# Gathered V rows and table blocks in separate pools, selection ended at slot 64, 58 table pairs beside the dots, high one-hots by one compare

## The chip, the cores and the metric

One Trainium2 chip (trn2), one of its NeuronCores. The metric is the device time of one execution in microseconds, lower is better. A NeuronCore has five engines that run their own instruction streams: TensorE (PE in the profile; PEld is its weight load), VectorE (DVE), ScalarE (ACT), GpSimd (POOL) and SyncE (SP), and 16 DMA engines that all of them share.

## The reference, cut to what matters

Two transformer-like blocks run over 256 tokens of 1024 numbers. The first (an mLSTM mixer, an MLP and a gated addition) and the first half of the second (forgetting attention, an RWKV-7 mixer, a layer norm) are not touched by the change. The last part is a product-key expert layer, `_peer`. Per block of 128 tokens:

```python
q = (xb @ w_q).reshape(t, PEER_HEADS, 2, PEER_HALF)
s = jnp.einsum('thpd,hpkd->thpk', q, sub_keys).astype(jnp.float32)
top_s, top_i = lax.top_k(s, K)                       # K = 16, 8 heads, 128 keys a half
cand_s = top_s[:, :, 0, :, None] + top_s[:, :, 1, None, :]
cand_i = top_i[:, :, 0, :, None] * PEER_N_KEYS + top_i[:, :, 1, None, :]
best_s, best_pos = lax.top_k(cand_s.reshape(t, PEER_HEADS, K * K), K)
idx = jnp.take_along_axis(cand_i.reshape(t, PEER_HEADS, K * K), best_pos, axis=-1)
gate = jax.nn.softmax(best_s, axis=-1).astype(xb.dtype)
h = jax.nn.gelu(jnp.einsum('thkd,td->thk', u_table[idx], xb), approximate=False)
return jnp.einsum('thk,thkd->td', gate * h, v_table[idx])
```

So each token picks 8 x 16 = 128 of 16384 experts; each pick is called a slot here. For every slot the dot of a row of U (1024 numbers, 4 KB) with the token gives a weight, and the output is the weighted sum of the same rows of V. A layer norm follows. All of it is float32.

## The kernel before, in words

The 256 tokens are two blocks, 0 and 1, of 128 tokens, one token per partition. The tail of the kernel has four stages; times are from the profile.

**Dots of block 0** (line 1507, to about 891 us) and **dots of block 1** (line 1590, 891 to 1147). A slot n gathers 128 rows of U, one per token, by an indirect DMA that GpSimd issues (`gather`, line 1376), and VectorE multiplies and sums them with the tokens in one instruction (`u_dot`, line 1404). For some slots of the early part TensorE does it instead (`u_mm`, line 1380, and `u_diag`). The row tiles come from `ub` (six tiles of 4 KB per partition) and, for block 1 and four slots of seven, from a tag `ust` of eight tiles in the pool `sec` (`u_tile`, line 1368). Beside the dots VectorE selects the experts of the heads to come (`select`, advanced in steps by `paced`). In block 1 the selection of the last six heads is spread to slot `SEL`. At that slot the pools `late` (the selection's) and `sec` are closed, and the one-hot tensor of block 1, `AT1`, is put in their place, 64 KB per partition. From then on rows have only the six tiles of `ub`.

**The dense product.** V isn't gathered for block 0, nor for the low half (columns 0 to 511) of block 1. There a weight matrix is built over all 16384 experts. An expert's index is 128 x high + low. For each token, the tensor `AT` holds at [low, token, high] the sum of weights; it is the product of a low one-hot and a weighted high one-hot over the token's 128 slots. ScalarE makes the low one-hots (`spread_low`, line 1425: four Squares and a Relu for a group of four tokens). `spread` (line 1432) does the rest for a group: VectorE compares the iota row with the high index and multiplies by the weight (line 1439, four instructions of 128x128, one per token), TensorE multiplies the two one-hots, ScalarE evicts. There are 32 groups per block. The matrix then multiplies blocks of the V table: a **pair** is 256 experts x 512 columns, 512 KB, and there are 64 pairs for each half of the columns. A float32 product of 128x128 by 128x512 is two passes on TensorE, so a pair is four passes for one token block.

- High half of V for block 0: `hload` (line 1556) loads a pair `wh`, `hdense` (line 1571) multiplies it and asks for the next. `H1` of the 64 pairs are asked for beside the dots of block 1, the others in the spreads of block 1 (line 1666). The tiles are from `wraw` (four tiles, through `h_tile`), two of a tag in `sec` for two of six pairs while it is open, and from `ub` after the dots (`late_h`).
- Low half of V for both blocks: the last stage, line 1721, 1216 to 1512 us: `vload` loads a pair `w`, `dense` multiplies it for block 0 and for block 1. The first six (`PRE`) come from `ub`; after them even pairs from `ub`, odd ones from `wraw`.
- High half of V for block 1: gathered. `v_load` (line 1452) gathers 128 half rows of 2 KB, two slots to one tile; `v_add` (line 1461) multiplies them by the weight and adds them on VectorE. Six are asked for ahead. 28 are added between the spreads of block 1 (from the fifth group on), 100 in the last stage. The tiles come from `wraw` up to the last stage, and from `ub` in it (`v_tile`, `paced_v`).

What sets the order: VectorE runs its instructions in the order written (`manual_schedule`, line 1237). For the other engines the tile framework works out an order when the kernel is built, in which an instruction or a load may stand ahead of ones that are written before it; it also hands out the tiles of a pool in that order, and sets the waits. On the chip each engine then runs its own list in order. So SyncE's list holds the loads of `wh` and `w`, GpSimd's the gathers, and a wait of one holds all behind it.

The end: after the adds, `low_half(0)` and `last_norm(0)` run beside the last six pairs of block 1, then `low_half(1)`, `last_norm(1)` and the output.

Of the kernel before, what the change touches and what calls it, by code (L numbers as in the profile page):

```python
# [18 lines left out]
S, D = 256, 1024  # L19
# [4 lines left out]
def block_kernel(ctx: ExitStack, tc: tile.TileContext, I, out):  # L24
# [7 lines left out]
    sm = ctx.enter_context(tc.tile_pool(name="sm", bufs=4, side="right"))  # L32
# [17 lines left out]
    def pb():  # L50
        return psB.tile([128, 512], F, tag="b", name="pb")
# [1380 lines left out]
    def spread(t, q, ns=128):  # L1432

        g = AT[t][:, q * 4:q * 4 + 4]
        ps = pb()
        for i in range(4):
            n = q * 4 + i
            e1 = gt_.tile([128, 128], F, tag="e1", name="e1")[:ns]
            V.tensor_scalar(e1, io[:ns], tr_all[t][:ns, 0, n:n + 1], tr_all[t][:ns, 2, n:n + 1],  # L1439
                            op0=OP.is_equal, op1=OP.mult)  # L1440
            T.matmul(ps[:, i * 128:(i + 1) * 128], lhsT=g[:ns, i], rhs=e1, start=True, stop=True)  # L1441
        A.activation(out=g, in_=ps.rearrange("p (t i) -> p t i", t=4), func=AF.Copy)


    vts, paced_v = {}, []

    def v_tile():
        if paced_v:
            return ub.tile([128, D], R, tag="u", name="v").bitcast(F)
        return h_tile("v")  # L1450

    def v_load(s):
        if not vts:
            w = v_tile()
            vts[1], v = w[:, 512:], w[:, :512]
        else:
            v = vts.pop(1)
        gather(v, vhalf, idx_v[1], s)
        return v
# [70 lines left out]
    gt_ = ctx.enter_context(tc.tile_pool(name="onehot", bufs=6, side="right"))  # L1530

    def h_tile(name):
        return wraw.tile([128, WF], F, tag="raw", name=name)[:, :D]
# [50 lines left out]
    SEL, LOW, HN = 83, 36, 38  # L1584

    H1 = 48
# [3 lines left out]
    for n in range(128):  # L1590
# [32 lines left out]
        if n > SEL:  # L1623
            for _ in range((n - SEL - 1) * 32 // (127 - SEL), (n - SEL) * 32 // (127 - SEL)):
                spread_next(spread_low, low1, 1)
# [5 lines left out]
    def vload(b):  # L1631
        if b >= PRE and b % 2:
            w = h_tile("w")
        else:
            w = ub.tile([128, D], R, tag="u", name="w").bitcast(F)
        wt[b] = w.rearrange("p (b c) -> p b c", b=2)
        nc.sync.dma_start(out=wt[b], in_=vtab[b * 256:(b + 1) * 256, 0:512].rearrange("(b p) c -> p b c", p=128))
# [40 lines left out]
    paced_v.append(1)  # L1678
# [93 lines left out]
```

## Time and profile before

| | |
|---|---|
| runs of the kernel before | median 1530.12 us of 3 (1524.57 to 1533.26) |
| the profiled execution | 1525.52 us device time, span 1523.7 us, mean granted clock 0.954 |
| busy, share of the span | PE 85%, DVE 65%, ACT 36%, POOL 29% |
| HBM read | 336.21 MB |
| chain, by engine | PE 52%, DMA 17%, DVE 13%, ACT 10%, issue 4%, POOL 2% |

The span runs from the first to the last instruction of one profiled execution; the device time has 1.8 us more. A row of a group view reads: line, engine, operation, tiles written and read, shape, count, then busy us and mean ns of one, then the engine's idle time just before these instructions and what ended it. "Granted clock" is TensorE's clock as granted, a share of 2.4 GHz. A tile's name is that in the code: `u` and `ust` are rows of U, `v` gathered half rows of V, `wh` and `w` pairs of the V table, `e` the high one-hot, `AT` the matrix, `jk` the dot.

### The profile page before, as it was taken

What the parts mean: (1) busy time and instruction counts of PE and PEld (TensorE: products, weight loads), DVE (VectorE), ACT (ScalarE), POOL (GpSimd) and SP (SyncE); (2) the same over time, 40 slices, a digit from 0 to 9 for tenths busy, and PEclk for the clock granted to TensorE, in tenths of its full rate; (3) what the DMA queues carried; (4) which work ended last, traced back from release to release, by engine and by line L of the source; (5) the groups of instructions that cost most, each with busy time, mean ns of one, the idle gap of its engine ahead of it and who ended that gap; (6) DMA issues with size and microseconds to landing.
All of it is one profiled execution on the core that took longest, in us unless ns stands there. A gap on an engine that the chain in (4) does not pass through costs nothing.

```text
span 1523.7 us, 20095 instructions
## 1 busy us (share of the span) xinstructions
PE 1297.5 (85%) x7068; PEld 1054.6 (69%) x7068; DVE 987.4 (65%) x2456; ACT 546.2 (36%) x1046; POOL 446.2 (29%) x420
## 2 busy tenths in 40 slices
PE   8999999999999999979987579955558988793955
PEld 7889899878987788869887568832226855462633
DVE  6778555576664766878999889998565943212123
ACT  6465544474556412312325964300097300000000
POOL 2000000000000000036787764565433564223231
PEclk9999999999999999989999789999999999896987
DMA  7435665655443300559999997799998776654732
GB/s 239 137 126 183 193 190 186 188 173 162 137 138 118 107 12 1 177 202 366 342 371 346 340 354 242 241 402 401 401 401 305 244 259 214 236 196 119 260 90 90
DMA packets 132820, 338.58 MB, mean 222 GB/s; under 512 B 11674, under 2 KB 15088, under 8 KB 132720
## 3 DMA queue, kind: packets, MB, share of 16 engines
q1 hardware_dynamic: 83680, 165.01, 33.0%
q0 software_dynamic: 48288, 170.98, 31.3%
q10 hardware_dynamic: 752, 1.31, 0.3%
q8 instruction: 56, 0.92, 0.3%
q14 instruction: 44, 0.36, 0.1%
HBM read 336.21 MB, written 1.05 MB: 221 GB/s over the span
## 4 chain that ended last, share of the span: by engine, by line
PE 52%; DMA 17%; DVE 13%; ACT 10%; issue 4%; POOL 2%; SPq 0%; DVEq 0%; ACTq 0%; POOLq 0%
DMA v<-in_peer_v_dram,idxv 9%; PE pa L217 7%; PE pa L219 7%; PE pa L218 7%; ACT AT L1429 5%; PE pa L1642 4%; DVE jk L1408 4%; PE pa L1396 3%; DMA u<-in_peer_u_dram,idxu 3%; PE pb L1441 2%; PE pb L217 2%; PE pb L219 2%; PE pb L218 2%; ACT AT L1430 2%; PE pa L1187 2%
## 5 line engine op out<-in xcount | busy, mean ns | idle before, releaser
L1642 PE MATMUL pa<-w,AT 128*128 128x512 f32 x512 | 235.4, 620 | 69.2 <-DMA w<-in_peer_v_dram 69.2
L212 DVE TENSOR_TENSOR w<-raw,w 128x1024 fp32r<-128x1024 f32 (+2 forms) x162 | 197.7, 1224 | 117.7 <-ACT w L211 117.0
L1642 PEld LDWEIGHTS pa<-w,AT 128*128 128x128 f32 x512 | 150.9, 297 | 148.8 <-DMA w<-in_peer_v_dram 73.5
L211 ACT ACTIVATE w<-raw 128x1024 fp32r<-128x1024 f32 (+2 forms) x164 | 172.8, 1061 | 168.5 <-PE pa L219 71.1
L1377 POOL DMA_INDIRECT u<-in_peer_u_dram,idxu x166 | 185.5, 1117 | 119.5 <-DVE jk L1408 55.5
L1464 DVE SCALAR_TENSOR_TENSOR xa<-v,c,xa 128x512 f32<-128x512 f32 x128 | 95.9, 749 | 191.5 <-DMA v<-in_peer_v_dram,idxv 190.8
L1408 DVE SCALAR_TENSOR_TENSOR jk<-u,xa 128x1024 bf16<-128x1024 f32 x147 | 179.1, 1218 | 40.9 <-DMA u<-in_peer_u_dram,idxu 40.5
L1579 PE MATMUL pa<-wh,AT 128*128 128x512 f32 x256 | 131.0, 636 | 70.7 <-DMA wh<-in_peer_v_dram 70.0
L1377 POOL DMA_INDIRECT v<-in_peer_v_dram,idxv x128 | 127.3, 995 | 216.4 <-DVE xa L1464 148.2
L1579 PEld LDWEIGHTS pa<-wh,AT 128*128 128x128 f32 x256 | 70.8, 299 | 119.0 <-DMA wh<-in_peer_v_dram 100.9
L1396 PE MATMUL pa<-xF,uT 128*128 128x128 f32 x800 | 112.1, 298 | 28.4 <-ACT uT L1393 26.1
L1396 PEld LDWEIGHTS pa<-xF,uT 128*128 128x128 f32 x800 | 102.4, 208 | 38.9 <-ACT uT L1393 38.6
L1377 POOL DMA_INDIRECT ust<-in_peer_u_dram,idxu x90 | 110.0, 1222 | 66.2 <-PE pb L1392 22.5
L1704 ACT ACTIVATE xa<-xa,nmu 128x512 f32<-128x512 f32 x3 | 2.1, 717 | 292.7 <-DVE nmu L1698 292.7
L94 POOL DMA_DIRECT2D ln_g<-in_ln_g_dram x2 | 1.1, 572 | 285.6 <-PE pb L1105 285.0
L1429 ACT ACTIVATE AT<-io,tr 128x128 f32<-128x128 f32 x256 | 82.2, 400 | 0.4 <-DVE jk L1408 0.3
L1439 DVE TENSOR_SCALAR e<-io,tr 128x128 f32<-128x128 f32 x256 | 74.4, 359 | 4.8 <-PE pb L1441 3.8
L217 PE MATMUL pb<-xt,w 128*128 128x256 f32 (+2 forms) x272 | 76.9, 283 | 0.0
L219 PE MATMUL pb<-xt,w 128*128 128x256 f32 (+2 forms) x272 | 76.5, 281 | 0.0
L218 PE MATMUL pb<-xt,w 128*128 128x256 f32 (+2 forms) x272 | 76.5, 281 | 0.0
L1441 PEld LDWEIGHTS pb<-e,AT 128*128 128x128 f32 x512 | 64.5, 191 | 12.4 <-issue 6.6
L1408 DVE SCALAR_TENSOR_TENSOR jk<-ust,xa 128x1024 bf16<-128x1024 f32 x59 | 71.7, 1216 | 1.8 <-DMA ust<-in_peer_u_dram,idxu 1.6
(532 smaller groups left out, 2729.3 us busy)
## 6 DMA issues: line engine op xcount, KB each, us to landing
raw<-in_mlp_w_dram SPq DMA_DIRECT2D x64, 512.0 KB, 3.6
wh<-in_peer_v_dram SPq DMA_DIRECT2D x64, 512.0 KB, 13.3
w<-in_peer_v_dram SPq DMA_DIRECT2D x64, 512.0 KB, 6.0
raw<-in_w_in_dram SPq DMA_DIRECT2D x38, 512.0 KB, 3.4
raw<-in_mlstm_w_in_dram SPq DMA_DIRECT2D x20, 512.0 KB, 3.7
AT<-in_peer_w_q_dram SPq DMA_DIRECT2D x12, 512.0 KB, 18.0
raw<-in_mlstm_w_out_dram SPq DMA_DIRECT2D x8, 512.0 KB, 3.7
raw<-in_ple_gate_w_dram SPq DMA_DIRECT2D x8, 512.0 KB, 3.7
```

Of the source, the lines that this page charges most:

```text
L211: A.activation(out=w1[:, :kn * cn], in_=raw[:, :kn * cn], func=AF.Copy)
L212: (eng or V).tensor_tensor(w2[:, :kn * cn], raw[:, :kn * cn], w1[:, :kn * cn].bitcast(F), op=OP.subtract)
L217: T.matmul(o, lhsT=a1, rhs=b1, start=start, stop=False)
L218: T.matmul(o, lhsT=a1, rhs=b2, start=False, stop=False)
L219: T.matmul(o, lhsT=a2, rhs=b1, start=False, stop=stop)
L1377: G.indirect_dma_start(out=dst, out_offset=None, in_=tab, in_offset=bass.IndirectOffsetOnAxis(ap=idx[:, s:s + 1], axis=0))
L1396: T.matmul(o[:, :128], lhsT=uT[:, k], rhs=xT[:, k], start=k == 0, stop=k == 7)
L1408: V.scalar_tensor_tensor(jk, u, 1.0, x2[:, t], op0=OP.mult, op1=OP.mult, accum_out=hd_all[t][:, s:s + 1])
L1429: A.activation(out=g[:, n], in_=io, func=AF.Square, bias=tr_all[t][:, 1, q * 4 + n:q * 4 + n + 1])
L1464: V.scalar_tensor_tensor(z, v, c_, z, op0=OP.mult, op1=OP.add)
L1579: T.matmul(acc2, lhsT=AT[0][:, :, n], rhs=w[:, i], start=n == 0, stop=n == 127)
L1642: T.matmul(acc[t], lhsT=AT[t][:, :, n], rhs=wt[b][:, i], start=n == 0, stop=n == 127)
```

## The change

Five edits of the tail. Gathered V rows always come from `wraw`, and all low-half pairs from `ub`. The second selection ends at slot 64 instead of 83, which closes `sec` and opens `AT1` there; the low one-hots of block 1 are then made over the 45 slots that follow. `H1` is 58 instead of 48. In 21 of the 32 groups of block 0 and 16 of block 1, `spread` makes one compare of 128x512 on VectorE, and ScalarE multiplies each of the four 128x128 parts by its weight; the other groups are as before. The pool `onehot` has two tiles of 128x512 instead of six of 128x128, and `sm` (small column values) three of each tag instead of four.

```diff
--- before.py
+++ after.py
@@ -29,7 +29,7 @@
     xap = ctx.enter_context(tc.tile_pool(name="xap", bufs=1))
     wst, xts = ExitStack(), ExitStack()
     const = ctx.enter_context(tc.tile_pool(name="const", bufs=1, side="right"))
-    sm = ctx.enter_context(tc.tile_pool(name="sm", bufs=4, side="right"))
+    sm = ctx.enter_context(tc.tile_pool(name="sm", bufs=3, side="right"))
     wraw = ctx.enter_context(tc.tile_pool(name="wraw", bufs=4, side="right"))
     WF = 1056
     rings = [(wst.enter_context(tc.tile_pool(name="wsp", bufs=3, side="right")), WF)]
@@ -1429,29 +1429,31 @@
             A.activation(out=g[:, n], in_=io, func=AF.Square, bias=tr_all[t][:, 1, q * 4 + n:q * 4 + n + 1])
         A.activation(out=g, in_=g, func=AF.Relu, scale=-1.0, bias=1.0)
 
-    def spread(t, q, ns=128):
+    def spread(t, q):
 
         g = AT[t][:, q * 4:q * 4 + 4]
         ps = pb()
+        e1 = gt_.tile([128, 4, 128], F, tag="e1", name="e1")
+        both = q % (3 if t == 0 else 2) == 0
+        if not both:
+            V.tensor_tensor(e1, tr_all[t][:, 0, q * 4:q * 4 + 4, None].to_broadcast([128, 4, 128]),
+                            io[:, None, :].to_broadcast([128, 4, 128]), op=OP.is_equal)
         for i in range(4):
             n = q * 4 + i
-            e1 = gt_.tile([128, 128], F, tag="e1", name="e1")[:ns]
-            V.tensor_scalar(e1, io[:ns], tr_all[t][:ns, 0, n:n + 1], tr_all[t][:ns, 2, n:n + 1],
-                            op0=OP.is_equal, op1=OP.mult)
-            T.matmul(ps[:, i * 128:(i + 1) * 128], lhsT=g[:ns, i], rhs=e1, start=True, stop=True)
+            c_ = tr_all[t][:, 2, n:n + 1]
+            if both:
+                V.tensor_scalar(e1[:, i], io, tr_all[t][:, 0, n:n + 1], c_, op0=OP.is_equal, op1=OP.mult)
+            else:
+                A.activation(out=e1[:, i], in_=e1[:, i], func=AF.Copy, scale=c_)
+            T.matmul(ps[:, i * 128:(i + 1) * 128], lhsT=g[:, i], rhs=e1[:, i], start=True, stop=True)
         A.activation(out=g, in_=ps.rearrange("p (t i) -> p t i", t=4), func=AF.Copy)
 
 
-    vts, paced_v = {}, []
-
-    def v_tile():
-        if paced_v:
-            return ub.tile([128, D], R, tag="u", name="v").bitcast(F)
-        return h_tile("v")
+    vts = {}
 
     def v_load(s):
         if not vts:
-            w = v_tile()
+            w = h_tile("v")
             vts[1], v = w[:, 512:], w[:, :512]
         else:
             v = vts.pop(1)
@@ -1527,7 +1529,7 @@
     uxx.close()
     xfx.close()
     qx.close()
-    gt_ = ctx.enter_context(tc.tile_pool(name="onehot", bufs=6, side="right"))
+    gt_ = ctx.enter_context(tc.tile_pool(name="onehot", bufs=2, side="right"))
 
     def h_tile(name):
         return wraw.tile([128, WF], F, tag="raw", name=name)[:, :D]
@@ -1581,9 +1583,9 @@
 
     late_h = []
     s2 = chain(*(select(1, h, 2) for h in (2, 4, 6)))
-    SEL, LOW, HN = 83, 36, 38
-
-    H1 = 48
+    SEL, LOW, HN = 64, 36, 38
+
+    H1 = 58
     MMS1 = range(1, LOW, 2)
 
     later = chain(paced(s2, TWO, 18), paced(s2, 2 * TWO, SEL - 18))
@@ -1621,7 +1623,7 @@
             for i in range(2):
                 slots_T(1, ex_all[1][:, i], i)
         if n > SEL:
-            for _ in range((n - SEL - 1) * 32 // (127 - SEL), (n - SEL) * 32 // (127 - SEL)):
+            for _ in range((n - SEL - 1) * 32 // 45, (n - SEL) * 32 // 45):
                 spread_next(spread_low, low1, 1)
     assert next(low0, None) is None and next(low1, None) is None and not due
     late_h.append(1)
@@ -1629,10 +1631,7 @@
     wt = {}
 
     def vload(b):
-        if b >= PRE and b % 2:
-            w = h_tile("w")
-        else:
-            w = ub.tile([128, D], R, tag="u", name="w").bitcast(F)
+        w = ub.tile([128, D], R, tag="u", name="w").bitcast(F)
         wt[b] = w.rearrange("p (b c) -> p b c", b=2)
         nc.sync.dma_start(out=wt[b], in_=vtab[b * 256:(b + 1) * 256, 0:512].rearrange("(b p) c -> p b c", p=128))
 
@@ -1675,7 +1674,6 @@
         vload(b)
     V.scalar_tensor_tensor(x2[:, 0, 512:], x2[:, 0, 512:], ALPHA, acc2, op0=OP.mult, op1=OP.add)
     V.bn_stats(out=st[:, 0, 1], in_=x2[:, 0, 512:])
-    paced_v.append(1)
     o2 = out[0].rearrange("(t p) d -> t p d", p=128)
 
     def low_half(t):
```

## Rows read from the trace of the kernel before

**Rows 1.** The page, part 4: the chain that ended last, by line.
```profile
DMA v<-in_peer_v_dram,idxv 9%; PE pa L217 7%; PE pa L219 7%; PE pa L218 7%; ACT AT L1429 5%; PE pa L1642 4%; DVE jk L1408 4%; PE pa L1396 3%; DMA u<-in_peer_u_dram,idxu 3%; PE pb L1441 2%; PE pb L217 2%; PE pb L219 2%; PE pb L218 2%; ACT AT L1430 2%; PE pa L1187 2%
```

**Rows 2.** Windows over the last third; the first line names the columns.
```profile
core 0: us, PE busy (x) PEld busy (x) DVE busy (x) ACT busy (x) POOL busy (x), PEclk, DMA share, GB/s
893.00:980.00 87.00, 82.99 (x683) 78.47 (x682) 82.57 (x307) 38.55 (x73) 48.93 (x44) 0.99 0.79 267
...
1034.00:1106.00 72.00, 39.92 (x78) 21.23 (x78) 47.94 (x86) 1.04 (x6) 32.23 (x34) 1.00 1.03 401
1106.00:1147.00 41.00, 23.18 (x45) 12.52 (x46) 24.79 (x42) 40.85 (x122) 14.09 (x15) 1.00 1.02 394
1147.00:1164.00 17.00, 13.96 (x34) 8.58 (x34) 1.08 (x5) 16.12 (x44) 7.63 (x8) 1.00 0.86 291
1164.00:1216.00 52.00, 52.00 (x305) 42.93 (x303) 51.72 (x155) 18.51 (x31) 25.63 (x26) 1.00 0.81 268
1216.00:1296.00 80.00, 67.14 (x151) 43.94 (x150) 32.23 (x44) 0.60 (x1) 40.27 (x38) 0.95 0.72 236
...
1384.00:1411.00 27.00, 0.43 (x2) 0.25 (x2) 7.08 (x10) 0.00 (x0) 9.77 (x10) 0.54 0.49 145
```

**Rows 3.** Timelines, 1195 to 1290 and 1340 to 1425: start, us, engine, what.
```profile
1235.83 44.98 PE L1642 MATMUL pa<-w,AT 128*128 128x512 f32 x100 [4.91 <-DMA w<-in_peer_v_dram]
...
1339.82 44.37 PE L1642 MATMUL pa<-w,AT 128*128 128x512 f32 x103
...
1380.13 0.95 POOL L1377 DMA_INDIRECT v<-in_peer_v_dram,idxv  x1 [3.64 <-DVE xa L1464]
...
1383.57 0.75 DVE L1464 SCALAR_TENSOR_TENSOR xa<-v,c,xa 128x512 f32<-128x512 f32 x1 [3.71 <-DMA v<-in_peer_v_dram,idxv]
1385.03 0.75 DVE L1464 SCALAR_TENSOR_TENSOR xa<-v,c,xa 128x512 f32<-128x512 f32 x1 [0.70 <-DMA v<-in_peer_v_dram,idxv]
1386.05 0.95 POOL L1377 DMA_INDIRECT v<-in_peer_v_dram,idxv  x1 [3.71 <-DVE xa L1464]
```

**Rows 4.** Groups of instructions, 1216 to 1512.6: busy us, mean ns, idle before.
```profile
L1642 PE MATMUL pa<-w,AT 128*128 128x512 f32 x498 | 227.5, 620 | 69.2 <-DMA w<-in_peer_v_dram 69.2
...
L1377 POOL DMA_INDIRECT v<-in_peer_v_dram,idxv x94 | 94.1, 1001 | 171.1 <-DVE xa L1464 148.2 <-issue 17.1 <-PE pa L1642 5.5
```

**Rows 5.** SyncE's own waits, 1190 to 1512: us in total, times, longest.
```profile
SPq L1637 <- DMA v<-in_peer_v_dram,idxv: 175.6, 19, 40.3
```

**Rows 6.** DMA queues, 1216 to 1512.6: packets, MB, share (q1 blocks, q0 rows).
```profile
q1 hardware_dynamic: 15963, 30.76, 30.7%
q0 software_dynamic: 7574, 24.80, 26.7%
```

**Rows 7.** Groups of instructions, 1147 to 1216.
```profile
L1579 PE MATMUL pa<-wh,AT 128*128 128x512 f32 x64 | 33.1, 630 | 0.9 <-DMA wh<-in_peer_v_dram 0.9
...
L1429 ACT ACTIVATE AT<-io,tr 128x128 f32<-128x128 f32 x31 | 9.8, 385 | 0.0
```

**Rows 8.** DMA, 980 to 1034 (first line) and 1034 to 1147: issues, KB, us to landing.
```profile
wh<-in_peer_v_dram SPq DMA_DIRECT2D x18, 512.0 KB, 20.5
...
q0 software_dynamic: 7845, 28.54, 64.0%
q1 hardware_dynamic: 8539, 16.45, 38.8%
...
u<-in_peer_u_dram,idxu POOLq DMA_INDIRECT x44, 10.5
```

**Rows 9.** Groups by shape, 893 to 980.
```profile
L1439 DVE TENSOR_SCALAR e<-io,tr 128x128 f32<-128x128 f32 x128 | 36.5, 351 | 3.7 <-PE pb L1441 3.6
...
L1408 DVE SCALAR_TENSOR_TENSOR jk<-ust,xa 128x1024 bf16<-128x1024 f32 x11 | 13.4, 1215 | 0.0
...
L1312 DVE TENSOR_TENSOR oh<-pf,io 128x512 f32<-128x512 f32 x2 | 1.4, 716 | 0.0
```

**Rows 10.** Line L1418, duration in ns min/median/max.
```profile
L1418 ACT ACTIVATE tr<-pb x6: 257/274/278, 825.5 to 1162.9; 128x128 f32<-128x128 f32 x6
```

## Prediction

> **What bounds the kernel now.** I read the page's chain first, then a table of windows over the last third, then each window alone. In the chain the largest single item is the landing of the gathered V rows, 9% of the span [rows 1]; they are gathered only after the dots, from about 1147 us. The windows say which engine each stretch lives on [rows 2]. From 893 to 980 us (the first dots of token block 1 beside the spreads of block 0) TensorE is busy 83.0 of 87 us and VectorE 82.6. From about 980 to 1147 the DMA engines are full: 401 GB/s at a share of 1.03, with TensorE half idle. From 1147 to 1216 (block 1's spreads) TensorE is busy 14.0 of 17 and then 52.0 of 52. From 1216 to 1512.6 (the dense product with the low half of V, for both blocks) nothing is full: 236 GB/s at a share of 0.72 in the first 80 us, and a stretch of 27 us, 1384 to 1411, in which TensorE works for 0.4 us.
>
> That last stage is the one to read closely. While TensorE runs, it runs evenly: 103 passes in 44.37 us, 0.431 us each [rows 3]. There are 498 passes in the stage; they are busy 227.5 us and idle 69.2, all of it waiting for table blocks [rows 4]. Why are the blocks late? SyncE, which loads them, stood 175.6 us on gathered rows [rows 5], and GpSimd, which gathers the rows, stood 148.2 us on VectorE's adds of rows [rows 4]. The timeline shows how: a gather starts at 1380.13, its row is added at 1383.57 as soon as it is there, and the next tile's gather starts at 1386.05, right after the second add, which began at 1385.03. One tile of two rows is in flight at a time, 5.9 us per tile, though the code asks for six rows ahead. Rows and even table blocks share the six tiles of `ub`; odd blocks share `wraw`. Blocks take the tiles that rows would need, then the next block waits for a row that is itself waiting for a tile, and TensorE stands.
>
> **The change part by part.** The sum is made against the profiled execution (span 1523.7 us, device time 1525.5). The median of the three runs, 1530.1, is 4.6 us above that; the last step adds it.
>
> *Pools of their own (last stage).* Blocks get all of `ub` (six tiles), rows all of `wraw` (four tiles, eight rows). A block then waits only for TensorE to release a block, a row only for VectorE to add the row eight before it. No chain runs through both. What is late next is TensorE: 498 passes x 0.431 = 214.6 us in place of 296.6, **-82 us**. Is DMA able to follow? In this stage the blocks took 30.7% and the rows 26.7% of the 16 engines over 296.6 us [rows 6]: 91 + 79 = 170 us of full DMA, less than 215. GpSimd's 94 gathers at 1.00 us [rows 4] and VectorE's adds at 0.75 [rows 3] need some 100 us at the least. By an estimate from these the rows finish in 150 us, and during that time DMA is nearly full (79 + 150/215 x 91 = 142 of 150 us). That costs something: from 1235.8, with rows and blocks both moving, 100 passes took 44.98 us, 0.450 each [rows 3]. About 250 passes at 0.019 more: **+5** (bounds 0 and the first rival).
>
> *58 pairs beside the dots.* In 1034 to 1147 DMA is full, so ten more 512 KB loads can't be taken in for nothing: at 400 GB/s they are 13 us. But the count 48 doesn't hold the loads back now. A load is issued whenever a tile is free, and 64 passes, that is 16 pairs, are left after 1147 [rows 7]: as many as 64 - 48, because DMA allowed no more. So I expect the dots to end when they do now, about 1147, with some 16 pairs still to come: 0, with bounds of -8 (VectorE's relief below lets DMA fill up earlier) and +10 (most of the 13 us falls before the last row).
>
> *Selection by slot 64.* VectorE gets the same selection in 46 slots instead of 65; the rows' prefetch is the cover, and DMA is the bound there, so 0. It lets the low one-hots of block 1 start some 19 slots earlier on ScalarE. Now ScalarE is the one that is late after the dots: 40.9 of 41 us and 16.1 of 17 busy around 1147 [rows 2]. That tail of about 13 us goes, but TensorE is late next: in those 17 us it idles only 3, as it has pairs to do. Gain 0 to 3. The price: from slot 65 on the row tiles shrink from 14 to the six of `ub`, and the streamed pairs from six tiles to four. That is how slots 84 to 127 run today, at 394 to 401 GB/s [rows 2], with a median landing of 10.5 us [rows 8]: (10.5 + 1.2 for the dot [rows 9]) / 6 = 2.0 us per slot, just the DMA pace. So 0. The two row loads for the last norm and the two transposes move along on GpSimd's and TensorE's queues; none is new.
>
> *One compare for four one-hots.* Four compares of 0.351 us (1.40) become one of 128x512; the nearest row, a broadcast is_equal of that size, takes 0.716 [rows 9]. VectorE saves 0.69 us in 21 of 32 groups of block 0 and 16 of block 1: 14 and 11 us. ScalarE gets four copies per group. No row shows one from SBUF with a per-row scale; a copy from PSUM takes 0.274 [rows 10], a Square from SBUF 0.385 [rows 7]. I take 0.33 (halfway), 28 us in the first 87 us, where it is busy 38.6, and 21 us in the second spread, where it has room. Since TensorE is busy 83.0 of 87 us in the first, the gain there is at most its idle 4 us: I take 0, bounds -4 and +5 (TensorE waiting in line behind the copies).
>
> *Block 1's spreads, 1147 to 1216.* TensorE does 66.0 of 69 us of work. The work stays. New is that the last six pairs of the high half now sit in `wraw`, where before they went to `ub`. The rows need `wraw` too, so the first rows are gathered only when pairs 60 to 63 have been multiplied. VectorE's order is as written, with the first row's add after the fifth spread: everything behind it (compares, so the spreads) waits for that row. TensorE has pairs left to do meanwhile and may take early blocks of the low half. I take **+6**, one landing of a row (3.4 us from gather to add, [rows 3]) and some of a second; bounds -3 (all idle time gone) and +25 (four tiles, each a landing and two adds late).
>
> The smaller pool of column vectors (3 for 4) covers one-column values of norms, far apart: 0.
>
> **Sum:** -82 + 5 + 6 = -71; 1523.7 - 71 = 1452.7 span, 1454.5 device time, and 1459 with the 4.6 us to the median.
>
> **Rivals.** *First, DMA turns hurt the blocks.* While both queues were full, from 1034 to 1147, the gather queue moved 7845 packets and the load queue 8539 [rows 8]: nearly equal turns. In the last stage rows and blocks both go in 2 KB pieces, so equal turns are half of the bytes each. At the rates of [rows 6] (30.8 MB in 91 us, 24.8 in 79: some 325 GB/s) half is 163 GB/s, a pair each 3.2 us, under the 3.45 that TensorE needs (8 passes): no loss. At the 236 GB/s that the first 80 us of the stage moved, half is 118: 94 rows of 262 KB take 209 us, a pair 4.44; 47 pairs in that time and 11 more at 3.45 (six are there at the start) make 247 us instead of 214.6 + 5, and the total is 1459 + 28 = 1487. For it: this is the only measured mixture. Against: it was not full (share 0.72). The Trainium skill, page "DMA: Bandwidth & Descriptors", section on queues, rings and completion order, says that each engine takes its queues in turn, packet by packet; the trace's near equal counts agree, so the page would let the free-running rows take half from the blocks.
>
> *Second, the change does not part the two:* a row's gather still waits for the add just before it. Then 47 tiles x 5.9 us = 277 us hold the stage, the end comes where it is now, and with +6 in the spreads the result is 1536. For it: the code already asked for six rows ahead and got one tile. Against: block 1's spreads gather from `wraw` alone, and there VectorE shows no wait for a row (busy 51.7 of 52).
>
> *Third, slower: six row tiles are too few from slot 65.* Landings are 10.5 us at the median late in the dots, but 20.5 for the streamed pairs from 980 to 1034 [rows 8]. If rows land in 20.5, a slot takes (20.5 + 1.2) / 6 = 3.6 us; 63 slots take 228 instead of 126 at 2.0, and the result is 1459 + 102 = 1561. It decides from 3.1 us per slot, a landing of 17.5 us. Against it: the second half of the dots runs with just these tiles today.
>
> **Numbers.** Forecast 0.74, first rival 0.14, second 0.05, third 0.03, the rest 0.04 for a better end than my bounds. The low end takes every lower bound: -82 - 3 - 4 - 8 = -97, 1433 for the median. The high end takes in the first rival: 1490. A measurement of this kernel can tell about 0.5%. Faster 0.92, same 0.03 (half of the second rival), slower 0.05.
>
> **What would show it.** Right: in the last stage TensorE has no wait for blocks over some us, 0.43 us per pass throughout, granted clock 1.0; SyncE waits for TensorE alone; adds of rows end well before the products. The dots end within 10 us of 1147, with about 16 pairs left. ScalarE's low one-hots end before the dots. The first add of a row shows a wait behind the last pairs. Wrong: adds of rows spread over the whole last stage; passes above 0.45 throughout; slots above 2.5 us after 64.

## The result, and the profile after

The changed kernel took 1453.32 us (median of 4 runs, 1450.03 to 1456.91), the kernel before on the same chip 1530.91 (4 runs): a ratio of 0.950, 95% interval 0.946 to 0.954. The profiled execution is 1450.03 us, span 1448.3, mean granted clock 0.975.

Ratios here and below leave out runs that took over 1.5% longer than the fastest of the same kernel, some of those on chip C; medians and ranges hold all runs.

The gain depends on the chip. The runs of the experiments fell on three, called B, C and D here in the order of their use; A is that of the two times above. The record doesn't number A, and by its times it may be D.

| chip | kernel before, median us | changed kernel, median us | ratio, 95% interval |
|---|---|---|---|
| A | 1530.91 (4 runs) | 1453.32 (4) | 0.950, 0.946 to 0.954 |
| B | 1552.68 (13) | not run | |
| C | 1544.70 (11) | 1526.04 (8) | 0.988, 0.984 to 0.992 |
| D | 1530.09 (7) | 1456.31 (4) | 0.952, 0.949 to 0.956 |

First what happened on A. Windows of the changed kernel, cut as in [rows 2] and with the same columns:

```profile
893.00:980.00 87.00, 82.65 (x687) 78.85 (x686) 78.08 (x265) 63.66 (x161) 48.37 (x43) 0.98 0.79 268
...
1034.00:1106.00 72.00, 41.44 (x78) 21.32 (x78) 43.17 (x70) 56.08 (x163) 36.83 (x35) 0.98 1.03 406
1106.00:1147.00 41.00, 24.36 (x44) 12.16 (x44) 25.90 (x42) 0.00 (x0) 17.93 (x19) 0.96 1.04 408
1147.00:1164.00 17.00, 13.68 (x30) 8.75 (x31) 4.00 (x7) 1.26 (x2) 0.00 (x0) 1.00 0.87 299
1164.00:1216.00 52.00, 44.91 (x244) 35.55 (x243) 37.32 (x88) 29.41 (x76) 27.54 (x28) 1.00 0.69 220
1216.00:1296.00 80.00, 76.31 (x216) 54.20 (x217) 50.02 (x76) 8.56 (x23) 61.17 (x57) 1.00 0.90 317
1296.00:1340.00 44.00, 44.00 (x104) 30.34 (x103) 23.34 (x31) 0.00 (x0) 34.25 (x33) 1.00 0.97 346
...
1384.00:1411.00 27.00, 27.00 (x64) 18.50 (x64) 0.00 (x0) 0.00 (x0) 0.00 (x0) 1.00 0.49 153
```

The stretch 1384 to 1411, in which TensorE had worked for 0.43 us, is full now: 64 passes in 27 us at clock 1.00. From 1296 to 1340 rows and blocks flow together at 346 GB/s and TensorE doesn't wait. The groups of the last stage (1227 to 1440), as [rows 4]:

```profile
L1641 PE MATMUL pa<-w,AT 128*128 128x512 f32 x488 | 209.8, 593 | 0.7 <-ACT AT L1449 0.7
...
L1377 POOL DMA_INDIRECT v<-in_peer_v_dram,idxv x93 | 100.3, 1078 | 28.4 <-issue 20.5 <-DVE xa L1466 5.5 <-DMA v<-in_peer_v_dram,idxv 2.4
L1466 DVE SCALAR_TENSOR_TENSOR xa<-v,c,xa 128x512 f32<-128x512 f32 x100 | 75.2, 752 | 59.6 <-DMA v<-in_peer_v_dram,idxv 58.0
```

TensorE's idle time before its passes fell from 69.2 us to 0.7, GpSimd's wait for the adds from 148.2 to 5.5. SyncE's own waits in the same stretch, as [rows 5]:

```profile
SPq L1636 <- PE pa L1641: 218.5, 58, 57.2
```

Before it, it had stood 175.6 us on gathered rows; now it waits for TensorE to free a block, and for no row. The chain of work that ended last tells the same in one piece, 488 passes at 0.430 us:

```profile
1227.41 209.82 PE pa L1641 x488
```

Where the 75.4 us of the span lie, by the ends of the stages in the two traces: the dots of block 1 end at 1152.8 instead of 1146.9 (+5.9), the last spread 73.9 us after that instead of 69.2 (+4.7), the last pass 210.5 us after that instead of 296.5 (-86.0). The tail is 11.1 us in both.

### The profile page after: what moved, and what is told of

Read it like the earlier page. It is cut to its first block, busy times and chain, and to the rows that moved or that the text cites. A ratio compares the mean times of both kernels' runs of the same rounds, so it can differ in the third digit from the quotient of the medians.

```text
span 1448.3 us, 20024 instructions
## 1 busy us (share of the span) xinstructions
PE 1290.2 (89%) x7068; PEld 1056.9 (73%) x7068; DVE 974.5 (67%) x2345; ACT 590.0 (41%) x1194; POOL 451.0 (31%) x420
## 4 chain that ended last, share of the span: by engine, by line
PE 69%; DMA 13%; ACT 9%; DVE 7%; issue 1%; SPq 0%; DVEq 0%; ACTq 0%
PE pa L1641 15%; DMA wh<-in_peer_v_dram 10%; PE pa L217 8%; PE pa L219 8%; PE pa L218 8%; PE pa L1396 4%; PE pb L1448 3%; PE pa L1581 3%; ACT AT L1429 3%; PE pb L217 2%; PE pb L219 2%; PE pb L218 2%; PE pa L1187 2%; PE pb L963 2%; DMA AT<-in_peer_w_q_dram 2%; ACT uT L1393 1%
## 5 line engine op out<-in xcount | busy, mean ns | idle before, releaser
L1377 POOL DMA_INDIRECT u<-in_peer_u_dram,idxu x178 | 198.2, 1113 | 126.6 <-DVE jk L1408 60.0
L1408 DVE SCALAR_TENSOR_TENSOR jk<-u,xa 128x1024 bf16<-128x1024 f32 x159 | 193.7, 1218 | 51.3 <-DMA u<-in_peer_u_dram,idxu 50.7
L1641 PE MATMUL pa<-w,AT 128*128 128x512 f32 x512 | 222.7, 595 | 1.0 <-ACT AT L1449 0.7
L1377 POOL DMA_INDIRECT v<-in_peer_v_dram,idxv x128 | 134.6, 1052 | 78.1 <-issue 25.4
L1377 POOL DMA_INDIRECT ust<-in_peer_u_dram,idxu x78 | 94.8, 1215 | 61.6 <-PE pb L1392 29.3
L1448 PE MATMUL pb<-e,AT 128*128 128x128 f32 x512 | 68.9, 280 | 11.6 <-ACT e L1447 11.5
L1448 PEld LDWEIGHTS pb<-e,AT 128*128 128x128 f32 x512 | 63.0, 191 | 17.2 <-ACT e L1447 14.1
L217 PE MATMUL pa<-w,xt 128*128 128x512 f32 x176 | 71.6, 412 | 1.4 <-ACT w L211 1.0
```

What stands on the lines that cost most here:

```text
L217: T.matmul(o, lhsT=a1, rhs=b1, start=start, stop=False)
L1377: G.indirect_dma_start(out=dst, out_offset=None, in_=tab, in_offset=bass.IndirectOffsetOnAxis(ap=idx[:, s:s + 1], axis=0))
L1408: V.scalar_tensor_tensor(jk, u, 1.0, x2[:, t], op0=OP.mult, op1=OP.mult, accum_out=hd_all[t][:, s:s + 1])
L1448: T.matmul(ps[:, i * 128:(i + 1) * 128], lhsT=g[:, i], rhs=e1[:, i], start=True, stop=True)
L1641: T.matmul(acc[t], lhsT=AT[t][:, :, n], rhs=wt[b][:, i], start=n == 0, stop=n == 127)
```

## The experiments

### The parting of the pools alone, and all but it (chip B)

pools_alone is the kernel before with the two pool edits and nothing else:

```diff
     def v_tile():
-        if paced_v:
-            return ub.tile([128, D], R, tag="u", name="v").bitcast(F)
         return h_tile("v")
@@
-        if b >= PRE and b % 2:
-            w = h_tile("w")
-        else:
-            w = ub.tile([128, D], R, tag="u", name="w").bitcast(F)
+        w = ub.tile([128, D], R, tag="u", name="w").bitcast(F)
```

> The kernel before with one edit: rows of V always from wraw, all low-half pairs from ub; 48 pairs, slot 83 and the old compares stay. Theory (the shared tiles alone made the last stage wait): the last stage falls from 296 to 210-220 us, 498 passes at 0.43, no wait of TensorE for blocks above a few us; the stages up to 1216 stay, so 1442 to 1455 us in all. Rival (the last stage needs the early freeing of ub by the 58 pairs as well): blocks are late at first, the last stage takes 235 us or more, 1465 us or more.

all_but_pools is the changed kernel with these two edits undone:

```diff
-            w = h_tile("v")
+            w = v_tile()
@@
-        w = ub.tile([128, D], R, tag="u", name="w").bitcast(F)
+        if b >= PRE and b % 2:
+            w = h_tile("w")
+        else:
+            w = ub.tile([128, D], R, tag="u", name="w").bitcast(F)
```

> The kernel after with the pools put back as before (rows from ub in the last stage, odd pairs from wraw); 58 pairs, slot 64 and the new compares stay. Theory: no gain without the pools, the last stage stays at 280 to 300 us, 1520 to 1545 us in all. Rival (the other edits carry a good part): 1500 us or less.

Measured: pools_alone 1532.69 us, ratio 0.987 (0.982 to 0.991); all_but_pools 1560.78 us, ratio 1.004 (1.002 to 1.007). The last stage of all_but_pools (groups, 1256 to 1551) has the old chain in full:

```profile
L1649 PE MATMUL pa<-w,AT 128*128 128x512 f32 x488 | 223.9, 622 | 72.1 <-DMA w<-in_peer_v_dram 71.4 <-ACT AT L1449 0.7
...
L1377 POOL DMA_INDIRECT v<-in_peer_v_dram,idxv x94 | 94.1, 1001 | 170.4 <-DVE xa L1471 143.1 <-issue 18.4 <-PE pa L1649 5.5
```

72.1 us idle for blocks against 69.2 [rows 4], 143.1 of waiting for adds against 148.2. (The time lies above the expected 1520 to 1545; the kernel before is 21.8 us slower on this chip than on A.) So without the parting the other four edits gain nothing here, if anything they cost 0.4%, and the parting removes the stall. But it brought 1.3% here, not 5%: the last stage of pools_alone took 270.7 us (1243.3 to 1514.0). That is in the range of its rival, but not for the rival's reason: no block is late at first, TensorE is full up to 1296. The windows of pools_alone and a stretch of its timeline show a loss that chip A hadn't:

```profile
1243.00:1296.00 53.00, 53.00 (x126) 36.51 (x125) 30.92 (x42) 0.60 (x1) 41.73 (x38) 1.00 0.90 307
1296.00:1340.00 44.00, 28.58 (x40) 11.15 (x39) 23.30 (x31) 0.00 (x0) 34.35 (x32) 0.70 0.77 237
1340.00:1384.00 44.00, 29.74 (x35) 10.36 (x35) 22.49 (x30) 0.00 (x0) 27.43 (x25) 0.56 0.76 239
1384.00:1411.00 27.00, 27.00 (x64) 18.49 (x64) 0.00 (x0) 0.00 (x0) 0.00 (x0) 1.00 0.52 171
```

```profile
1301.96 1.23 PE L1637 MATMUL pa<-w,AT 128*128 128x512 f32 x2 [0.94 <-issue]
...
1303.62 0.59 PE L1637 MATMUL pa<-w,AT 128*128 128x512 f32 x1 [0.43 <-issue]
...
1305.76 0.59 PE L1637 MATMUL pa<-w,AT 128*128 128x512 f32 x1 [1.55 <-issue]
...
1319.25 1.01 PE L1637 MATMUL pa<-w,AT 128*128 128x512 f32 x1 [1.82 <-issue]
```

From about 1300 until the rows end near 1380, many passes come one at a time, 0.7, 1.4, 2.1 or 2.8 us apart, where on A each follows in 0.43. They wait for "issue", nothing that the profile shows. The granted clock of 0.70 and 0.56, means over times at 2.4 and at 1.2 GHz, fell after such gaps had begun and isn't enough: 44 us hold 102 passes of 0.43 at full clock, at 0.70 and 0.56 that would be 72 and 57, and 40 and 35 are there. As soon as no row flows, 64 passes take 27 us again. TensorE isn't the only engine held up so: VectorE's adds of rows begin late too with nothing to wait for, up to 2.6 us (1256 to 1400, us in total, times, longest), where the changed kernel on A and D shows no such wait of either engine:

```profile
PE pa L1637 <- issue: 29.4, 37, 1.8
...
DVE xa L1462 <- issue: 15.6, 17, 2.6
```

### The other ways of giving out the tiles (chip B)

pools_swapped leaves the rows in `ub` and puts all blocks from the seventh on in `wraw`; rows_with_odd puts the rows into `wraw` beside the odd blocks and leaves the even blocks in `ub`.

```diff
-        if b >= PRE and b % 2:
+        if b >= PRE:
             w = h_tile("w")
```

> The kernel before, parted the other way in the last stage: rows keep ub (six tiles), all pairs from the seventh on come from wraw (four tiles). Theory (it is the sharing, not how many tiles): last stage 210 to 225 us, about 1450 us in all; four tiles hold two pairs in use and two on their way, so TensorE may wait a little. Rival (six tiles for the pairs is what counts): TensorE waits for pairs all through, 240 us or more, 1480 us or more.

```diff
     def v_tile():
-        if paced_v:
-            return ub.tile([128, D], R, tag="u", name="v").bitcast(F)
         return h_tile("v")
```

> The kernel before with half of the parting: rows from wraw in the last stage too, where the odd pairs stay; even pairs have ub alone. Theory (any shared pool ties them): one tile of rows in flight and long waits again, last stage 270 to 310 us, 1500 to 1540 us in all. Rival (it was the six tiles of ub that were short, now three more are free): last stage below 240 us, 1470 us or less.

Measured in one run each: 1541.00 and 1563.58 us, against 1552.68; the last stage took 284.8 and 305.2 us. With half of the blocks still sharing the rows' pool, the chain stays; groups of rows_with_odd, 1256 to 1528:

```profile
L1640 PE MATMUL pa<-w,AT 128*128 128x512 f32 x439 | 198.8, 616 | 55.9 <-DMA w<-in_peer_v_dram 55.9
...
L1377 POOL DMA_INDIRECT v<-in_peer_v_dram,idxv x87 | 84.2, 967 | 186.6 <-DVE xa L1462 163.3 <-issue 20.9 <-DMA v<-in_peer_v_dram,idxv 2.4
```

GpSimd waits 163.3 us for adds, and the rows end at 1529.5, not at 1381.9 as in pools_swapped. In pools_swapped, where rows and blocks are parted too but the blocks have four tiles, GpSimd waits 2.7 us for adds; TensorE idles 29.8 us for blocks and 24.0 on "issue". So it is the sharing that makes GpSimd wait for adds, not which pool is whose. In time pools_swapped missed its expectation (210 to 225 us for the stage) and came out at its rival's; it took 14.1 us longer in the stage than pools_alone, so six tiles seem to serve the blocks better than four, but with one run and slow passes in both that isn't shown.

### The other edits, one at a time (chip C)

after_again is the changed kernel as it is, pools_again the same kernel as pools_alone. after_h1_48 has `H1 = 48` again; after_old_compares has `spread` as before, with six one-hot tiles of 128x128.

```diff
-    H1 = 58
+    H1 = 48
```

```diff
-        e1 = gt_.tile([128, 4, 128], F, tag="e1", name="e1")
...
+            e1 = gt_.tile([128, 128], F, tag="e1", name="e1")[:ns]
+            V.tensor_scalar(e1, io[:ns], tr_all[t][:ns, 0, n:n + 1], tr_all[t][:ns, 2, n:n + 1],
+                            op0=OP.is_equal, op1=OP.mult)
...
-    gt_ = ctx.enter_context(tc.tile_pool(name="onehot", bufs=2, side="right"))
+    gt_ = ctx.enter_context(tc.tile_pool(name="onehot", bufs=6, side="right"))
```

> The changed kernel once more, beside the others of this call on one chip, since the kernel before differs by 22 us between the chips of the first two calls. Theory A (the pools alone carry the gain, and the chip of the earlier call slows any kernel in which rows and blocks flow together): here it is within 10 us of the pools-alone kernel of this call, and its last stage has the same slow stretch if that one has it. Theory B (the pools need the other edits): 40 us or more below the pools-alone kernel, with an even last stage of 205 to 220 us.

> The kernel before with the pools edit alone, again, beside the changed kernel. Theory A: the ratio to the kernel before is that of the changed kernel within 1%. Theory B: about 0.985 again, the changed kernel about 0.95.

> The changed kernel with 48 pairs asked for beside the dots instead of 58: the last ten pairs of the high half take ub after the dots, and the first blocks of the low half wait for them. Theory A: within 10 us of the changed kernel. Theory B, if it is the pairs that the pools need: near the pools-alone kernel, 40 us or more above the changed one.

> The changed kernel with the old high one-hots (four compares on VectorE per group, six small tiles). The forecast gave this edit 0: within 5 us of the changed kernel. If VectorE's pace sets the spreads of block 1, they end later by up to 11 us (16 groups, 0.69 us each); if ScalarE's copies held TensorE up in block 0's spreads, the dots end earlier by up to 5.

Measured (kernel before 1544.70), with the ends of the stages in the profiled executions:

| kernel | median us (range) | ratio, 95% interval | dots end | last spread | last pass |
|---|---|---|---|---|---|
| after_again | 1526.04 (1516.37 to 1547.51) | 0.988, 0.984 to 0.992 | 1177.5 | 1255.3 | 1514.5 |
| pools_again | 1509.45 (1486.08 to 1523.53) | none | 1167.0 | 1236.5 | 1490.8 |
| after_h1_48 | 1512.58 (1498.49 to 1531.35) | 0.977, 0.969 to 0.984 | 1170.1 | 1230.6 | 1496.1 |
| after_old_compares | 1523.25 (1504.04 to 1534.74) | 0.978, 0.972 to 0.983 | not used | | |

The scatter is wide, and the last stage takes 254.3 to 265.5 us in the three profiles, so only the larger steps count. None of the other edits earns time here. The pools alone came out no slower than the whole change: 16.6 us below it by the medians, so neither within the 10 us of Theory A nor 40 us above as Theory B had it. With `H1` at 48 the interval just meets that of after_again. Its dots end 7.5 us earlier and its spreads 24.7 us earlier, but `H1` did only part of this. The last dot of block 0, when both kernels have asked for the same six pairs, already comes 7.0 us earlier (897.7 against 904.7), and the dots of block 1 then take 272.4 us against 272.9, with 52.5 pairs done at their end against 53.3. The difference comes after the dots: the first spread begins 6.4 us after the last dot with 48 pairs and 26.4 us after it with 58, the last one ends 60.5 us after it against 77.7. With the old compares the interval lies just below that of after_again, by 1% in the middle; where the difference arises isn't known. The slow passes are in the three profiles too; windows of after_again (1256 to 1296, then 1296 to 1384):

```profile
1256.00:1296.00 40.00, 40.00 (x93) 27.60 (x94) 23.41 (x32) 0.00 (x0) 31.03 (x30) 1.00 0.96 345
1296.00:1384.00 88.00, 66.71 (x107) 30.66 (x105) 47.85 (x64) 0.00 (x0) 69.11 (x63) 0.79 0.79 246
```

107 passes in 88 us, where A had 208. The first of these lines excludes the simplest cause, the DMA load by itself: rows and blocks together at 345 GB/s, and TensorE full.

### Rows paced, rows moved, rows without GpSimd (chip D)

after_third is the changed kernel again. row_adds_paced makes VectorE touch each second block before it adds the rows of that round, so rows can't run ahead of the blocks:

```diff
+            p_ = sm.tile([128, 1], F, tag="pace", name="pace")
+            V.tensor_copy(p_, wt[b][:, 0, :1])
             for _ in range((b // 2 + 1) * VN // 31 - b // 2 * VN // 31):
                 v_next()
```

paced_no_rows_in_spreads has that too, and adds no row between the spreads:

```diff
         if q % 2 == 0:
             hdense()
-        if q >= 4:
-            v_next()
```

rows_by_plain_loads loads the rows of the last stage with another queue; these are not the chosen rows, so that part of the sum is another:

```diff
+        if by_load:
+            nc.scalar.dma_start(out=v, in_=vtab[s * 128:(s + 1) * 128, 512:])
+        else:
-        gather(v, vhalf, idx_v[1], s)
+            gather(v, vhalf, idx_v[1], s)
```

> The changed kernel once more, the baseline for the three that go with it. Two chips have shown TensorE's passes 0.7 to 2.8 us apart while rows and blocks flow at once (some 90 us, ended by the last row's add); the first chip showed 0.43 us all through. If this chip is like those two: a last stage of about 250 to 270 us and a ratio to the kernel before of 0.985 to 0.99. If it is like the first: 210 us and 0.95.

> The changed kernel, but before the rows of each round of the last loop (two blocks) VectorE reads one column of the first of these blocks, so rows are added, and gathered, at the pace of the blocks: 3.2 rows in the 6.9 us that TensorE takes for two blocks, all through the stage instead of in its first 135 us. Theory A, the slow passes need rows and blocks together at the full DMA rate (340 us and over in GB/s terms): with rows at half of that rate the passes are 0.43 us apart everywhere and the last stage takes 210 to 225 us on any chip, so 25 to 50 us less than the changed kernel where that shows the slow passes, the same within 5 us where it doesn't. Theory B, they come with gathers beside blocks at any rate: the slow passes are spread over the whole stage and the time is no better. Theory C, they belong to a time of the program (some 1290 to 1390 us), whatever the rows do: the same stretch, the same loss.

> As the paced kernel, and no rows between the spreads of block 1: all 128 are added in the last stage, 4.1 in 6.9 us. If the spreads of block 1 are bound by VectorE (compares 0.7 us and over, 28 adds of 0.7 us) and by the first rows, which wait for tiles of the last pairs, the spreads end some 10 to 15 us earlier than in the paced kernel and the time falls by as much, less what TensorE did of the low half meanwhile (24 passes, 10 us): 0 to 10 us less. If the blocks in these spreads hold them (the first one took 10.7 us to land), no gain.

> The changed kernel, but the rows added in the last stage come by plain loads that ScalarE's queue issues, 128 consecutive half rows of the table at a time, in place of GpSimd's gathers: the same bytes and the same adds, but not the chosen rows, so that part of the sum is another. If the slow passes come from the total DMA load, they remain (passes 0.7 us and more apart until the last row's add). If they come from GpSimd's gathers (their descriptors, or GpSimd's own accesses), they vanish and the last stage takes 210 to 220 us.

Measured (kernel before 1530.09): after_third 1456.31 us, ratio 0.952 (0.949 to 0.956); row_adds_paced 1457.45, 0.952 (0.949 to 0.956); paced_no_rows_in_spreads 1457.28, 0.951 (0.948 to 0.955); rows_by_plain_loads 1476.88 in one run. Chip D is like A: 198 passes in 84 us with the rows at full rate. So neither the pacing nor the plain loads met slow passes to remove, and whether they would remove them on B or C stays open. The pacing costs nothing.

Leaving the rows out of the spreads didn't shorten them either, 50.9 us from first to last (1185.2 to 1236.1) as against 51.4 in after_third: so the expectation that VectorE's work binds them falls. The waits point elsewhere; paced_no_rows_in_spreads, 1186 to 1236 (us in total, times, longest):

```profile
DVE e L1439 <- PE pb L1448: 19.4, 15, 1.6
...
PE pb L1448 <- ACT e L1447: 9.8, 10, 1.0
```

VectorE waits for the product two groups earlier to free a one-hot tile, and TensorE waits for ScalarE's copies of the next one: with two tiles, compare, copies and product follow each other in a ring of some 3.2 us for two groups (50.9 us for 32). The waits of 9.8 us for ScalarE are the same in the changed kernel.

rows_by_plain_loads shows rows that crowd out the blocks, which is what the first rival feared. First a window and the DMA queues (1256 to 1340) of after_third; rows come on q0, blocks on q1:

```profile
1256.00:1296.00 40.00, 40.00 (x94) 27.41 (x94) 21.41 (x29) 0.00 (x0) 31.15 (x30) 1.00 0.96 346
```

```profile
q0 software_dynamic: 4816, 15.78, 52.3%
q1 hardware_dynamic: 6727, 12.97, 43.7%
```

Then windows and the same queues of rows_by_plain_loads, rows on q10, and TensorE's group from 1227 to 1440:

```profile
1256.00:1296.00 40.00, 35.36 (x78) 22.18 (x77) 27.39 (x38) 0.00 (x0) 0.00 (x0) 1.00 0.99 346
1296.00:1340.00 44.00, 38.38 (x80) 22.55 (x78) 31.82 (x43) 0.00 (x0) 0.00 (x0) 0.96 1.02 367
```

```profile
q10 hardware_dynamic: 11166, 20.32, 65.8%
q1 hardware_dynamic: 4991, 9.63, 34.2%
```

```profile
L1644 PE MATMUL pa<-w,AT 128*128 128x512 f32 x435 | 195.0, 605 | 11.9 <-DMA w<-in_peer_v_dram 11.1 <-ACT AT L1449 0.7
```

Over these 84 us gathered rows took 188 GB/s and left the blocks 154, just the 152 that TensorE uses (0.524 MB each 3.44 us). Plain loads took 242 and left 115; TensorE waited for blocks, and the last stage grew from 210.5 to 229.7 us: 11.1 us of this is the wait, the rest are passes at 0.446 us instead of 0.430. What keeps the rows from hurting the blocks in the changed kernel is, most likely, GpSimd's own pace, one gather per 1.38 us (61 in 84 us). That isn't shown apart from the kind of queue, which is another too; no run gathers faster or loads more slowly.

## Why the prediction was right, and where not

It forecast 1459 us (1433 to 1490) with 0.92 for faster; measured 1453.32 on A and 1456.31 on D. The range doesn't hold the 1526 of chip C: what happens there is none of its cases. Term by term, on A:

- *Pools, -82 and +5.* Right in mechanism. The stage is 86.0 us shorter, of which 9 passes (24 instead of 15 are begun before the end of the last spread) make 3.9; that leaves the -82. The +5 for contention was mis-sized: a pass took 0.430 us beside the rows, as without them, so 0. Its source was misread. The 0.450 us of the 100 passes from 1235.8 on is the mean over a start at a lower granted clock, after a wait of 4.91 us, and passes at full pace with rows still flowing; in the kernel before:

```profile
1236.00:1250.00 14.00, 14.00 (x29) 8.72 (x30) 7.01 (x10) 0.00 (x0) 9.13 (x9) 0.88 0.78 251
1250.00:1265.00 15.00, 15.00 (x36) 10.32 (x36) 5.79 (x8) 0.00 (x0) 8.05 (x8) 1.00 0.74 240
```

  The first stretch has 29 passes in 14 us at clock 0.88 (0.483 each), the second 36 in 15 at clock 1.00 (0.417), at nearly the same DMA rate.
- *58 pairs, 0.* Right for the dots: on C they took 272.4 us with 48 pairs and 272.9 with 58, and with 48 asked for 52.5 were done, so the count doesn't hold the pairs back, as forecast. "With some 16 pairs still to come" failed: some 10 were left, but by another edit (next item). The count has its price in the spreads (below).
- *Selection by slot 64, 0 to -3.* The step that failed is a 0 for the dots, most likely this one. From the last dot of block 0 they took 265.0 us instead of 260.1 (+4.9 of the +5.9; the rest was there before), and 4 to 6 us more on B and C too with the other edits than without (275.3 against 269.7 to 271.1; 272.9 and 272.4 against 267.2; one profile each, and those of the same code on D lie 3.3 apart). So it is neither the pools nor the count. 53.8 pairs are done at their end instead of 48.0; 5.8 pairs are 3.0 MB, at 400 GB/s 7.6 us of DMA time. They were gained early: from 980 to 1034, at the same total rate, the pairs' queue (q1) took from the rows' (q0). Before, then changed:

```profile
q0 software_dynamic: 3709, 13.49, 64.8%
q1 hardware_dynamic: 3654, 7.06, 35.6%
...
q0 software_dynamic: 3173, 11.56, 55.8%
q1 hardware_dynamic: 4691, 9.05, 44.7%
```

  Of the three edits left the end of the selection is the likeliest cause, since rows lose eight of their 14 tiles by it; no run parts it from the compares and the smaller pools, so this isn't shown. ScalarE did its low one-hots before 1106 and stood still to 1147, as forecast. Rows of U landed in 10.2 us at the median from 1034 to 1147 (10.5 before), so the third rival, which needs 17.5, didn't come. The gain didn't show either: after the dots TensorE had other things to wait for.
- *Compares, 0.* The spreads of block 0 took 83.3 us (896.9 to 980.2), 82.9 before. The copies are dearer than the 0.33 taken, by the median of this view:

```profile
L1447 ACT ACTIVATE e<-e,tr x148: 384/390/413, 897.8 to 1225.8; 128x128 f32<-128x128 f32 x148
```

- *Block 1's spreads, +6.* Measured +4.7 from the end of the dots, but the place was another. Rows did wait for pairs, as said (GpSimd's first gather stood 24.9 us, until 1167.2), but their adds held nothing: TensorE did. The timeline of the changed kernel:

```profile
1163.15 8.96 PE L1581 MATMUL pa<-wh,AT 128*128 128x512 f32 x20 [1.34 <-DMA wh<-in_peer_v_dram]
1165.87 4.02 SPq L1636 DMA_DIRECT2D w<-in_peer_v_dram  x6
1167.23 0.96 POOL L1377 DMA_INDIRECT v<-in_peer_v_dram,idxv  x1 [24.91 <-PE pa L1581]
...
1172.29 2.09 PE L1641 MATMUL pa<-w,AT 128*128 128x512 f32 x4 [0.18 <-DMA w<-in_peer_v_dram]
...
1174.21 0.27 PE L1417 MATMUL pb<-ident,c 128*128 128x128 f32 x1
...
1174.52 0.28 ACT L1418 ACTIVATE tr<-pb 128x128 f32<-128x128 f32 x1 [20.39 <-PE pb L1417]
1174.84 1.11 DVE L1445 TENSOR_SCALAR e<-io,tr 128x128 f32<-128x128 f32 x4 [21.33 <-ACT tr L1418]
```

  The transpose that gives the spreads their weights (L1417) was ready to run soon after the dots, but in TensorE's list it stands behind the last pairs and the first block, and the first block stands behind those pairs in SyncE's. So the first spread began at 1175.3, 22.5 us after the dots, where it had been 16.8. On C it is the 58 pairs that put it there: with 48 in the changed kernel the first spread began 6.4 us after the dots, not 26.4.
- *The sum.* -82 + 5 + 6 = -71 forecast; -86.0 + 4.7 + 5.9 = -75.4 measured. The two smaller steps that failed (+5 for contention, 0 for the dots) have opposite signs, so part of the closeness is luck.

Of the rivals, the second (one tile in flight still) would have needed GpSimd to wait for adds, and it did so for 5.5 us. The first didn't come, and rows_by_plain_loads shows why it was no idle fear: free-running rows left a block each 4.57 us (0.524 MB at 115 GB/s), the rival had worked out 4.44. That the two are close is luck: the rival took half of 236 GB/s, the run gave the blocks a third of 357. Nor do gathered rows go in the 2 KB pieces that the rival took: in [rows 6] they are 24.80 MB in 7574 packets, 3.3 KB each on average, against 1.9 KB for the blocks, so that equal turns would have given them more than half. The Trainium skill, page "DMA: Bandwidth & Descriptors", section on queues, rings and completion order, has each engine take its queues in turn; in that run the rows' queue moved 11166 packets to 4991 of the blocks'. No run shows how long either queue had work standing, so this neither bears out equal turns nor speaks against them.

What stays open: why passes come singly on B and C while rows flow. It isn't the block's landing alone, since a block is waited for once and gaps stand between passes of one block; it isn't the DMA rate alone, which was 345 GB/s just before; it isn't TensorE or its clock alone, since VectorE's adds are held up too. On B, all_but_pools and rows_with_odd, whose rows flow at about half the rate, show no such passes. On B and C the 128th dot of block 0 also ends 8 to 19 us later than on A and D (897.7 to 905.4 against 886.8 to 889.8), long before the changed stage, so something else is slower there. The two kernels of chip C that came out about 1% under the changed one, with 48 pairs or the old compares, and the pools alone, were not run on a chip like A. So whether an edit undone would gain there stays open too, and that the pools alone give the whole 5% there is argued from the traces, not measured; on D no kernel tried was faster than the changed one.

## What to carry to other kernels

When a stage has nothing full and yet a gap, look for two streams that share a ring of tiles: a load that waits for a tile of the other stream chains the two, however many loads the code asks ahead. Part the rings first, before adding overlap elsewhere; here one such edit removed the stall, and four others that relieved engines off the bound brought no gain: on B nothing without it, on C nothing beyond it. And ask of each stream that becomes free what paces it: a gather that its issuing engine holds to one per 1.4 us leaves room that plain loads took.

## What the runs showed of the hardware

- The same kernel gave 0.950 and 0.952 of the time before on A and D and 0.988 on C, with the kernel before itself up to 1.5% apart between chips. One chip's interval (0.946 to 0.954) says nothing about that.
- TensorE's passes can stand 0.7 to 2.8 us apart with no wait in the profile to name, at mean granted clocks of 0.56 to 0.79, for some 90 us, and run at 0.43 directly before and after. VectorE's adds are held up in the same stretch.
- Rows by plain loads at 242 GB/s starved the blocks at a DMA share of 0.99 to 1.02; gathers at 188 GB/s beside the same blocks, at 0.96, cost TensorE nothing.
